# Six different byte offsets for the split weights of the narrow products

## The chip, the cores and the metric

The kernel runs on one core of a Trainium2 chip. The metric is the device time of one execution in microseconds (us). Before the change three runs gave 1155.51, 1155.75 and 1159.62 us, median 1155.75 us. About 0.5% (5.8 us) is what a measurement of this kernel can tell from no change.

## The reference

A decoder trunk of two layers over 512 tokens of width 1024, in float32. The first layer mixes with a gated delta rule, the second with sliding-window attention, both also attend to 256 memory tokens. Each layer ends in a gated feed-forward block, and this block is the part that matters here:

```
def swiglu(h, w_gate_up, w_down):
    gu = h @ w_gate_up
    return (jax.nn.silu(gu[..., :D_FF]) * gu[..., D_FF:]) @ w_down

x = x + swiglu(rms_norm(x, ln_ffn[layer]), w_gate_up[layer], w_down[layer])
```

D_FF is 2816, so the block has 22 column tiles of 128 for the gate and 22 for the up projection, and `w_down` goes back to 1024.

## The kernel before, in words

**Precision by three products.** TensorE multiplies in the type fp32r, which holds fewer bits than float32. So every float32 operand is split into a high part (ScalarE copies it to fp32r, line 148) and a low part (VectorE subtracts the high part from the original, line 161). `mm3` (line 206) then issues three matmuls for each 128x128 block of weights: high weight with high activation, high weight with low activation, low weight with high activation. Each matmul has its own load of 128 weight columns into the array (LDWEIGHTS), and it streams its moving operand, the activations, past them. In the trace both carry line 154, the load as PEld and the stream as PE.

**Wide and narrow matmuls.** Most projections stream 512 tokens per matmul (`project`, line 214, and the down projections). Most of the gate and up projections of the feed-forward block are done in another way: `quarters` (line 1005) multiplies two column tiles at once with seven smaller products in place of eight. Each of these seven products (`product`, line 1020) takes 512 columns of split weights (four blocks of 128) and streams 256 tokens, so it issues 4 x 3 = 12 narrow matmuls of 256 columns. Each half of each layer's block calls `quarters` ten times, 40 calls in all, hence 40 x 7 x 12 = 3360 narrow matmuls. The moving operands are halves of the normalised activations (`h`, `l`) and of sums of them, made by `token_sums` (line 979) and held in tiles that are called `T`.

**The ring.** The split weights of one product take 512 columns of a high tile and 512 of a low tile. `ffn` (line 870) takes three such pairs of tiles of 1024 + 64 columns from the pool (`parts`, line 190) and cuts each in two, which makes six places; `ring` (line 893) hands them out in turn, one for each product. With seven products per call and six places every place serves each of the seven kinds of product in turn. A place is free for ScalarE's next split when the 12 matmuls that read it are done.

**Where the bytes lie.** Tiles are padded to 64 bytes (line 104). In the built program every tile of moving operands of these products, and every weight tile, starts at 192 bytes modulo 256 in its row of on-chip memory (SBUF); halves of 256 tokens are 1024 bytes, blocks of 128 weight columns 512 bytes, so both keep that remainder. Before the change a ring part starts at column `SHIFT` = 52 of its tile, 208 bytes further, which puts it 48 bytes below its moving operand modulo 256. All other split weights are read from column 0: their distance to the moving operands is 0.

The work of one feed-forward block runs in this order: four gate tiles as wide products, then the narrow products without a break, then half of the down projection (wide), then the same again for the second half.

Of the kernel before, what the change touches and what calls it, by code (L numbers as in the profile page):

```python
# [19 lines left out]
T = 512  # L20
# [7 lines left out]
FT = DFF // P  # L28
EPS = 1e-6
LINE = 64  # L30
SHIFT, SPARE = 52, 64
NEG = -1e30
BASE = 32
NB = P // BASE
# [54 lines left out]
class Builder:  # L89
# [780 lines left out]
    def ffn(self, fp, xp, layer, h, apool, rope=False):  # L870
# [3 lines left out]
        acts, sums, open_pairs, places = [], [], [], []  # L874
# [18 lines left out]
        def ring():  # L893

            if not places:
                for _ in range(3):
                    two = self.parts()
                    places.extend(tuple(x[:, SHIFT + i * T:SHIFT + (i + 1) * T] for x in two) for i in range(2))
            places.append(places.pop(0))
            return places[-1]  # L900

        def begin(f, up, by, tag, bufs, then):

            o = [self.t(fp, [P, T], F32, tag, bufs) for _ in range(2)]
            steps = self.quarters(fp, [col(f + i, up) for i in range(2)], sums, by, o, ring)
            next(steps)
            end()
            next(steps)
            open_pairs.append((steps, then, o))
            return o  # L910
# [42 lines left out]
        if tail < KD:  # L953
# [9 lines left out]
            for t in parts:  # L963
                acc = self.acc[:, t]
                for m in range(tail, KD):
# [3 lines left out]
                    x = self.x[m][:, t]  # L969
# [301 lines left out]
```

## Time and profile before

| | |
|---|---|
| median of 3 runs | 1155.75 us |
| profiled execution, its own time | 1153.46 us |
| its span from the first to the last instruction | 1151.7 us |
| granted TensorE clock | 0.998 |
| TensorE streaming, share of the span | 98% |
| VectorE, ScalarE, GpSimd, share of the span | 73%, 55%, 7% |

One execution was recorded by the hardware profiler. PE is TensorE streaming matmuls, PEld the weight loads beside it, DVE is VectorE, ACT ScalarE, POOL GpSimd, SP the queue that issues most transfers. Matmuls overlap in the pipeline: a row's mean duration holds the latency from the first column in to the last one out, so what a stream of matmuls costs is read from the distance between their starts (called the pitch below), not from their durations. The chain of waits follows the program back from its last instruction; a row of it that holds many matmuls one after another, with the time from the first to the last, gives the mean pitch directly.

### The profile page before, as it was taken

The numbers are of one execution on the slowest core, as the hardware profiler recorded it, in microseconds if no ns is written. First come the engines' busy times: TensorE is split into PE (matmuls) and PEld (weight loads), VectorE is DVE, ScalarE is ACT, GpSimd is POOL, SyncE is SP. The second block draws the span as 40 slices with busy tenths as digits, with TensorE's granted clock in tenths as the row PEclk, the third lists the DMA queues.
The fourth block names the chain that finished last, engine by engine and source line by source line (L and its number), as shares of the span: only waits on it lengthen the run. The fifth ranks groups of instructions, "written<-read, shape, count | busy, mean of one in ns | idle before, by whom it ended". The sixth has DMA issues, their size and how long they took to land.

```text
span 1151.7 us, 19665 instructions
## 1 busy us (share of the span) xinstructions
PE 1129.2 (98%) x7476; PEld 990.3 (86%) x7476; DVE 842.4 (73%) x1587; ACT 632.1 (55%) x1271; POOL 86.1 (7%) x97
## 2 busy tenths in 40 slices
PE   7999999999999999999999999999999999999996
PEld 6888778887889998899998777778899988999986
DVE  5764877767789987389876767859799843898754
ACT  7579563366566652256654547675566622566533
POOL 0220000000111100011100000010011100111000
PEclk9999999999999999999999999999999999999999
DMA  8333342235557754567723421144478743577232
GB/s 310 118 121 110 120 101 95 85 106 162 167 138 186 191 126 127 160 147 187 181 69 103 134 79 38 40 110 129 115 186 193 180 112 103 147 190 184 70 95 93
DMA packets 73971, 152.83 MB, mean 133 GB/s; under 512 B 17756, under 2 KB 18420, under 8 KB 73876
## 3 DMA queue, kind: packets, MB, share of 16 engines
q1 hardware_dynamic: 62356, 130.59, 36.5%
q0 software_dynamic: 11520, 20.98, 11.6%
q8 instruction: 59, 0.97, 0.4%
q14 instruction: 36, 0.29, 0.1%
HBM read 144.58 MB, written 6.96 MB: 132 GB/s over the span
## 4 chain that ended last, share of the span: by engine, by line
PE 89%; DVE 6%; ACT 3%; DMA 1%; issue 1%; SPq 0%; DVEq 0%; ACTq 0%
PE pj L154 43%; PE g L154 38%; PE sc L154 5%; DVE wlo L161 2%; ACT sm L142 1%; PE pt L158 1%; PE qk L154 1%; ACT whi L148 1%; PE g L158 1%; DMA wraw<-in_wmk 1%; DVE stats L778 1%; DVE l L164 0%; DMA wraw<-in_win 0%; DVE x L164 0%; DVE btmp L161 0%
## 5 line engine op out<-in xcount | busy, mean ns | idle before, releaser
L148 ACT ACTIVATE whi<-wraw 128x512 fp32r<-128x512 f32 (+2 forms) x331 | 244.1, 746 | 253.6 <-PE pj L154 156.3
L161 DVE TENSOR_TENSOR wlo<-wraw,whi 128x512 fp32r<-128x512 f32 (+2 forms) x331 | 274.5, 839 | 104.7 <-ACT whi L148 98.4
L154 PE MATMUL pj<-h,whi 128*128 128x512 f32 (+1 forms) x676 | 266.4, 396 | 0.0
L154 PE MATMUL pj<-l,whi 128*128 128x512 f32 (+1 forms) x676 | 264.7, 392 | 0.4 <-DVE l L164 0.4
L154 PE MATMUL pj<-h,wlo 128*128 128x512 f32 (+1 forms) x676 | 264.0, 391 | 0.0
L154 PE MATMUL g<-T,whi 128*128 128x256 f32 x1280 | 228.1, 278 | 0.2
L154 PEld LDWEIGHTS g<-T,whi 128*128 128x128 f32 x1280 | 194.7, 188 | 1.8 <-DVE fu L164 1.8
L154 PE MATMUL g<-T,wlo 128*128 128x256 f32 x640 | 177.8, 278 | 0.0
L154 PEld LDWEIGHTS pj<-h,whi 128*128 128x128 f32 x676 | 126.8, 188 | 29.4 <-issue 3.6
L154 PEld LDWEIGHTS pj<-l,whi 128*128 128x128 f32 x676 | 127.1, 188 | 27.3 <-issue 1.8
L154 PEld LDWEIGHTS pj<-h,wlo 128*128 128x128 f32 x676 | 127.0, 188 | 25.7 <-issue 0.8
L154 PE MATMUL g<-l,whi 128*128 128x256 f32 (+1 forms) x508 | 144.4, 284 | 0.0
L154 PE MATMUL g<-h,whi 128*128 128x256 f32 (+1 forms) x508 | 144.3, 284 | 0.0
L154 PE MATMUL g<-h,wlo 128*128 128x256 f32 (+1 forms) x508 | 144.3, 284 | 0.0
L154 PEld LDWEIGHTS g<-T,wlo 128*128 128x128 f32 x640 | 120.1, 188 | 0.0
L154 PEld LDWEIGHTS g<-l,whi 128*128 128x128 f32 x508 | 95.3, 188 | 1.4 <-issue 0.2
L154 PEld LDWEIGHTS g<-h,whi 128*128 128x128 f32 x508 | 95.3, 188 | 1.2
L154 PEld LDWEIGHTS g<-h,wlo 128*128 128x128 f32 x508 | 95.3, 188 | 1.0
L1014 POOL DMA_DIRECT2D ws<-in_wgu x40 | 35.1, 877 | 707.9 <-DMA ws<-in_wgu 255.1
L148 ACT ACTIVATE whi<-ws 128x512 fp32r<-128x512 f32 x80 | 50.4, 630 | 49.0 <-PE g L154 40.2
L161 DVE TENSOR_TENSOR fu<-pj,rstd 128x512 f32<-128x512 f32 (+1 forms) x34 | 22.4, 660 | 54.2 <-PE pj L154 54.2
L161 DVE TENSOR_TENSOR wlo<-ws,whi 128x512 fp32r<-128x512 f32 x80 | 54.9, 686 | 6.4 <-ACT whi L148 6.3
(345 smaller groups left out, 1620.7 us busy)
## 6 DMA issues: line engine op xcount, KB each, us to landing
wraw<-in_wgu SPq DMA_DIRECT2D x48, 512.0 KB, 4.3
ws<-in_wgu SPq DMA_DIRECT2D x80, 256.0 KB, 3.5
ws<-in_wgu POOLq DMA_DIRECT2D x80, 256.0 KB, 4.7
wraw<-in_wdn SPq DMA_DIRECT2D x48, 384.0 KB, 3.1
wraw<-in_win SPq DMA_DIRECT2D x26, 512.0 KB, 3.6
wraw<-in_wgu SPq DMA_DIRECT2D x40, 256.0 KB, 4.5
wraw<-in_wout SPq DMA_DIRECT2D x16, 512.0 KB, 3.6
wraw<-in_wdn SPq DMA_DIRECT2D x16, 256.0 KB, 2.7
```

Source lines behind the costliest of these rows:

```text
L142: ins = self.nc.scalar.activation(out, in_, func, **kw).ins
L148: self.copied = self.nc.scalar.activation(out, in_, AF.Copy, **kw).ins
L154: return self.nc.tensor.matmul(out, lhsT, rhs, start=start, stop=stop, skip_group_check=more).ins
L158: return self.nc.tensor.transpose(out, in_, self.ident[:k, :k]).ins
L161: return eng.tensor_tensor(out=out, in0=a, in1=b, op=op).ins
L778: nc.vector.tensor_reduce(out=mx[:, i:i + 2], in_=ps[b], op=ALU.max, axis=AX.X)
L1014: nc.gpsimd.dma_start(s1, a22, accum_op=ALU.add)
```

## The change

The one shift of all six ring places becomes a shift of its own for each: 46, 55, 42, 53, 51 and 57 columns of 4 bytes, in the order in which the places are handed out. A part at column c starts 4c bytes above the start of its tile, so 256 - 4c bytes below its moving operand modulo 256: 72, 36, 88, 44, 52 and 28 bytes in place of 48 for all. High and low part of a place have the same distance.

```
-SHIFT, SPARE = 52, 64
+NARROW, SPARE = ((46, 55), (42, 53), (51, 57)), 64
...
             if not places:
-                for _ in range(3):
+                for shifts in NARROW:
                     two = self.parts()
-                    places.extend(tuple(x[:, SHIFT + i * T:SHIFT + (i + 1) * T] for x in two) for i in range(2))
+                    places.extend(tuple(x[:, o + i * T:o + (i + 1) * T] for x in two) for i, o in enumerate(shifts))
             places.append(places.pop(0))
             return places[-1]
```

The tiles have the same size and the same base address as before, and the instructions of each engine stand in the same order, row for row, with the same operands. Of the 3360 narrow matmuls 576 each then read weights at 72, 36, 88 and 44 bytes, and 528 each at 52 and 28. Before, all parts start at a multiple of 16 bytes; after, none does (remainders 8, 12, 8, 4, 12 and 4, as 192 + 4c modulo 16).

## The prediction

> **What bounds the kernel now.** I read the page's busy times first.
>
> ```profile
> span 1151.7 us, 19665 instructions
> PE 1129.2 (98%) x7476; PEld 990.3 (86%) x7476; DVE 842.4 (73%) x1587; ACT 632.1 (55%) x1271; POOL 86.1 (7%) x97
> ```
>
> TensorE is busy 98% of the span, so the question is whether the narrow matmuls wait for something or follow each other as fast as they can. The chain of waits answers it; its rows give start, length, work and count.
>
> ```profile
> 333.36 96.60 PE g L154 x828
> ...
> 432.74 64.17 PE pj L154 x283
> ...
> 823.50 96.60 PE g L154 x828
> ...
> 922.89 64.20 PE pj L154 x283
> ```
>
> The g rows are narrow matmuls, two of the four stretches with a ring. They lie in the chain unbroken: 828 matmuls in 96.60 us, 116.7 ns from start to start. The pj rows are wide ones (512 columns, distance 0): 64.20 us / 283 = 226.9 ns. What the helpers do in the same four stretches stands in the table of busy times by stretch (columns: sum of PE, PE, PEld, DVE, ACT, POOL, granted clock, share of the transfer engines, GB/s).
>
> ```profile
> 333.20:429.80 96.60, 96.60 (x830) 96.60 (x828) 86.31 (x156) 61.30 (x117) 12.97 (x15) 1.00 0.70 170
> 496.80:593.30 96.50, 96.50 (x829) 96.50 (x828) 84.89 (x152) 61.98 (x117) 13.00 (x15) 1.00 0.65 157
> 823.30:920.00 96.70, 96.70 (x830) 96.66 (x830) 85.81 (x154) 61.21 (x117) 16.46 (x19) 1.00 0.75 181
> 986.90:1083.50 96.60, 96.60 (x829) 96.57 (x828) 84.94 (x152) 61.99 (x117) 12.98 (x15) 1.00 0.64 157
> ```
>
> The clock is granted in full, VectorE is busy 85 to 86 us of 96.6, ScalarE 62. Who is ahead is seen in the groups by shape: the two rows of ScalarE that make high parts of 512 columns.
>
> ```profile
> L148 ACT ACTIVATE whi<-wraw 128x512 fp32r<-128x512 f32 x217 | 133.9, 629 | 84.8 <-PE g L154 38.1 <-PE pj L154 36.4 <-ACT fs L148 2.4
> L148 ACT ACTIVATE whi<-ws 128x512 fp32r<-128x512 f32 x80 | 50.4, 630 | 49.0 <-PE g L154 40.2 <-ACT fs L148 8.8
> ```
>
> Their idle time ends most often with a narrow matmul: the splits wait for a free place, TensorE does not wait for the splits. So the pitch of 3360 narrow matmuls is paid in full, 1 ns of it is 3.36 us of the kernel.
>
> **Does the offset matter at all?** This kernel has narrow matmuls at distance 0 too, those of the memory keys. The timeline shows them one by one; these are the first and the last of 40 in a row (start in us, then the modelled duration).
>
> ```profile
> 29.79 0.28 PE L154 MATMUL sc<-mh,wlo 128*128 128x256 f32 x1
> ...
> 34.47 0.28 PE L154 MATMUL sc<-mh,wlo 128*128 128x256 f32 x1
> ```
>
> 4.68 us over 39 steps is 120.0 ns. So at distance 0 the pitch is 120.0, at 48 it is 116.7. Now split that number. A wide matmul streams 256 more columns than a narrow one, and at distance 0 costs 226.9 - 120.0 = 106.9 ns more, which is the price of streaming 256 columns. What is left per matmul is an overhead of 120.0 - 106.9 = 13.1 ns at distance 0 and 116.7 - 106.9 = 9.8 ns at distance 48. That the distance makes this difference is an inference: the two groups also differ in stage and tiles, but have the same shapes, loads and types.
>
> The smallest overhead of a load that I find is in the transposes of the attention, whose moving operand is a constant: eight loads of 128 columns in a row.
>
> ```profile
> 757.33 0.90 PEld L158 LDWEIGHTS pt<-consts,sm 128*128 128x128 f32 x8 [0.60 <-ACT pf L148]
> L158 PEld LDWEIGHTS pt<-consts,sm 128*128 128x128 f32 x116 | 12.5, 140 | 6.5 <-ACT pf L148 2.7 <-issue 2.0 <-PE pj L154 0.8
> ```
>
> The second row gives 140 ns for one, so seven steps take 0.90 - 0.14 = 0.76 us, 109 ns each. That is the end below: a narrow matmul has to load 128 columns as well, so I take no pitch under 109.
>
> The end above comes from wide matmuls at distance 0 in another stage, first and last of ten.
>
> ```profile
> 80.27 0.40 PE L154 MATMUL pj<-l,whi 128*128 128x512 f32 x1
> ...
> 82.36 0.39 PE L154 MATMUL pj<-l,whi 128*128 128x512 f32 x1
> ```
>
> 2.09 us / 9 = 232.2 ns, 5.3 more than the 226.9 above at the same distance. So the pitch isn't fixed by the distance alone; the streams can also fall into a worse step with each other. The end above is 120.0 + 5.3 = 125.3 ns.
>
> **The change part by part.** Nothing is removed, added or moved in any engine's order; three things change address.
>
> *Splits that write the ring.* ScalarE and VectorE now write to starts that are not multiples of 16 bytes. VectorE has rows of that kind: the taps of the convolution write at 4, 8 and 12 bytes past an aligned start.
>
> ```profile
> L164 DVE SCALAR_TENSOR_TENSOR l<-x,gains,h 128x512 fp32r<-128x512 f32 x32 | 23.5, 748 | 1.5 <-ACT h L148 1.5
> L164 DVE SCALAR_TENSOR_TENSOR qv<-pj,gains,qv 128x511 f32<-128x511 f32 x12 | 9.0, 747 | 2.7 <-ACT qv L148 2.4
> L164 DVE SCALAR_TENSOR_TENSOR qv<-pj,gains,qv 128x509 f32<-128x509 f32 x12 | 8.9, 741 | 0.1
> ```
>
> 747 and 741 ns against 748 at an aligned start: no price. For ScalarE no row shows it. If a split took 10% more, 70 of them in a stretch would add 70 x 0.063 = 4.4 us to 62 busy ones of 96.6, which the idle rest covers. I cost this part at nothing. Without that cover it would be those 4.4 us in each of four stretches.
>
> *Weight loads of the ring.* This is the price that decides. The trace has a steady pitch at distances 0 and 48 only, for none of the six new ones. I assume that the effect repeats every 64 bytes, so that 64 is like 0 (an assumption; no row shows it), and draw straight lines between 120.0 at 0, 116.7 at 48 and 120.0 at 64, a difference of 3.3 ns. Distance 28 then gives +1.4 ns against 48, 36 gives +0.8, 44 +0.3, 52 +0.8; 72 counts as 8 and gives +2.8, 88 counts as 24 and gives +1.7. With the counts: 528 x (1.4 + 0.8) + 576 x (0.8 + 0.3 + 2.8 + 1.7) = 1162 + 3226 ns = 4.4 us. The mean pitch becomes 116.7 + 4.4 / 3.36 = 118.0 ns. Between the ends, 3360 x (109 - 116.7) = -25.9 us and 3360 x (125.3 - 116.7) = +28.9 us, I take this value because four of the six distances lie within 20 bytes of the measured 48 and the pitch there should resemble it.
>
> *Hand-over between products.* Every 12 matmuls the distance now jumps. Before it jumps from 48 to 0 where a stretch ends; these are the wide matmuls right behind the first stretch, the first and the fifth.
>
> ```profile
> 429.80 0.40 PE L154 MATMUL pj<-h,whi 128*128 128x512 f32 x1
> ...
> 430.71 0.39 PE L154 MATMUL pj<-l,whi 128*128 128x512 f32 x1
> ```
>
> Four steps take 0.91 us, by the rounding of the two starts at most 0.92; four steps of 226.9 ns are 0.908. A jump costs nothing to some 10 ns, 280 of them 0 to 2.8 us. Jumps of 8 to 52 bytes should cost less than this one, and some may help; I leave it out of the sum and in the range.
>
> The sum: 1153.46 + 4.4 = 1157.9 us for the profiled execution. The median of the three runs lies 2.3 us above that execution; 1155.75 + 4.4 gives 1160 us. That is 0.4%, inside 0.5% (5.8 us, what a measurement of this kernel can tell from no change).
>
> **A rule weighed.** The rows have 120.0 against 116.7 ns where shapes and types agree and the placement differs. The Trainium skill, page "TensorE: Matmul & The Clock Gate", section "Step-by-step: what each phase is for", says that TensorE has two independent read ports on SBUF, so that loading the next weights takes no bandwidth from the running matmul. By that the placement would change nothing and the time would stay at 1155.75 us. The two rows speak against it, as far as they differ in nothing else.
>
> Another one speaks against this change. The page "SBUF — State Buffer", section "Specifications (TRN2)", gives lines of 16 bytes and a penalty for each crossing to a new line. 512 bytes of weights that start off a line touch 33 lines, not 32; my estimate from this page and the overhead of 9.8 ns over 32 lines is 0.3 ns a matmul, 1 us in all. No run so far shows it.
>
> **The rivals.**
>
> *Slower: 48 is a good place and its neighbours are not.* If the 3.3 ns at 48 depend on whole 16-byte steps between the two streams, all six places, none of which is a multiple of 16 away, fall back to the 120.0 ns of distance 0: 3360 x 3.3 = 11.1 us, 1167 us. For it: 120.0 ns is exact over 39 steps, and the 232 ns row shows that worse steps exist. Against it: 48 to 44 and 52 is a small move. It decides against my forecast once the mean pitch passes 116.7 + 5.8 / 3.36 = 118.4 ns, which is only 0.4 above the forecast.
>
> *Faster: shifted by a part of 16 bytes the two streams stop meeting.* Parts that start 4 or 12 bytes off a multiple of 16 (36, 44, 52 and 28, 2208 matmuls) would come down to the 109 ns of the loads that meet nothing: 2208 x 7.7 = 17.0 us, 1139 us; half of it gives 1147 us. VectorE, at 86 us a stretch, would still fit in the 92 us left. For it: an overhead of 9.8 ns is there to be gained. Against it: no row shows a load at such an offset, and the two placements seen moved the pitch by 3 ns, not 8.
>
> *Nothing: the placement doesn't matter,* and the 3.3 ns come from the stage. Then 1155.75 us. For it: the two groups differ in stage. Against it: the narrow row holds 120.0 without spread, with the same shapes.
>
> **How the numbers follow.** Forecast (mean pitch 116.0 to 118.4) 0.39; nothing 0.06; slower rival and what lies above 118.4 ns 0.33; faster rival 0.22. So faster by over 0.5%: 0.22; within: 0.39 + 0.06 = 0.45; slower: 0.33. The range reaches from the half-way case of the faster rival, 1147 us, to the slower one with a microsecond on top, 1168 us; about 0.1 is left out at each end. The forecast alone would have 1153.4 to 1161.5: 3360 x (116.0 - 116.7) = -2.4 us and 3360 x (118.4 - 116.7) = 5.7 us from the median.
>
> **What would show it.** In the profile after, each of the four stretches of 828 narrow matmuls in the chain gives the mean pitch: 97.7 us is my forecast, 99.4 the slower rival, 92.4 or less the faster one, 96.6 no effect. Within a stretch the starts of 12 matmuls of a product show the pitch of each place: I expect the places at 72 and 88 slowest, 44 nearest to 116.7. A pitch off the line at 72 and 88 alone would fell the assumption of 64 bytes; 120 at 44 and 52 would prove the slower rival. ScalarE's rows for high parts should stay near 630 ns, VectorE's low parts near 690; PE waits in the stretches should stay absent. If the time moves while the pitch stays at 116.7, I have named the wrong resource.

## The result, and the profile after

The changed kernel took 1164.26, 1165.07 and 1166.47 us, median 1165.07 us, against 1155.75 us before: a ratio of 1.0082 with a 95% interval of 1.0062 to 1.0102. It is slower by 9.3 us, inside the predicted range of 1147 to 1168 us, but beyond the 5.8 us that the forecast of 1160 us still called no change. The profiled execution took 1166.47 us.

The page's busy times, as before:

```profile
span 1164.7 us, 19665 instructions
PE 1140.2 (98%) x7476; PEld 1001.0 (86%) x7476; DVE 845.7 (73%) x1587; ACT 632.3 (54%) x1271; POOL 86.0 (7%) x97
```

The span grew by 13.0 us, TensorE's busy time by 11.0, the helpers' by 3.3 and 0.2. The chain of waits shows where: the four stretches of narrow matmuls (start, length, work, count), with one wide stretch between them for comparison.

```profile
333.45 99.30 PE g L154 x828
435.51 64.16 PE pj L154 x283
499.67 99.30 PE g L154 x828
...
831.33 99.30 PE g L154 x828
...
997.54 99.30 PE g L154 x828
```

A stretch takes 99.30 us in place of 96.60; the wide one, whose addresses the change leaves alone, 64.16 as before. 99.30 / 828 = 119.9 ns is the new mean pitch, and 4 x 2.70 = 10.8 us is what the stretches add. The table of busy times by stretch has TensorE without a gap still, at a full clock (two of the four rows):

```profile
333.40:432.80 99.40, 99.40 (x830) 99.38 (x829) 87.49 (x156) 61.55 (x118) 12.94 (x15) 1.00 0.68 166
831.30:930.70 99.40, 99.40 (x830) 99.36 (x829) 86.90 (x154) 61.39 (x118) 16.42 (x19) 1.00 0.74 179
```

The splits into the shifted parts cost what they did, 630 and 633 ns on ScalarE, and still wait for places:

```profile
L148 ACT ACTIVATE whi<-wraw 128x512 fp32r<-128x512 f32 x217 | 135.5, 630 | 92.2 <-PE g L154 45.8 <-PE pj L154 35.4 <-ACT fs L148 2.5
L148 ACT ACTIVATE whi<-ws 128x512 fp32r<-128x512 f32 x80 | 50.6, 633 | 54.1 <-PE g L154 44.5 <-ACT fs L148 9.6
```

So TensorE itself runs slower, without waiting for anyone. Inside a product the pitch of each place is seen in the timeline; these are the first and the twelfth matmul of a product from the place at 52 bytes.

```profile
347.60 0.29 PE L154 MATMUL g<-h,whi 128*128 128x256 f32 x1
...
348.96 0.29 PE L154 MATMUL g<-h,wlo 128*128 128x256 f32 x1
```

1.36 us over 11 steps is 123 ns. Averaged over all products of a place, with the step to the next product, the starts give 119.7 ns at 28 bytes, 121.4 at 36, 117.5 at 44, 123.0 at 52, 118.1 at 72 and 119.9 at 88.

Outside the stretches the profiled execution lost 2.2 us more (13.0 - 10.8). The three executions of the changed kernel differ by as much among themselves, and the fastest of them, 1164.26 us, lies 10.8 us above the profiled one before. In the profile ScalarE waited longer for the output weights, in the row of that wait (us in total, times, longest) first before and then after:

```profile
ACT whi L148 <- DMA wraw<-in_wout: 8.2, 4, 2.9
```

```profile
ACT whi L148 <- DMA wraw<-in_wout: 10.6, 4, 4.4
```

That total lay between 4.2 and 10.4 us in the profiles of the experiments below, in no relation to their pitch. Why it differs, and whether it is what the 2.2 us are made of, stays open.

### The profile page after: what moved, and what is told of

Same layout as the page of the kernel before. It is cut to its first block, busy times and chain, and to the rows that moved or that the text cites. A ratio compares the mean times of both kernels' runs of the same rounds, so it can differ in the third digit from the quotient of the medians.

```text
span 1164.7 us, 19665 instructions
## 1 busy us (share of the span) xinstructions
PE 1140.2 (98%) x7476; PEld 1001.0 (86%) x7476; DVE 845.7 (73%) x1587; ACT 632.3 (54%) x1271; POOL 86.0 (7%) x97
## 4 chain that ended last, share of the span: by engine, by line
PE 87%; DVE 6%; ACT 3%; DMA 2%; issue 1%; SPq 0%; DVEq 0%; ACTq 0%
PE pj L154 41%; PE g L154 38%; PE sc L154 6%; DVE wlo L161 2%; ACT sm L142 1%; PE pt L158 1%; DMA wraw<-in_wout 1%; PE qk L154 1%; ACT whi L148 1%; PE g L158 1%; DVE l L164 1%; DMA wraw<-in_wmk 1%; DVE stats L778 1%; DVE T L161 0%; DVE x L161 0%
## 5 line engine op out<-in xcount | busy, mean ns | idle before, releaser
L161 DVE TENSOR_TENSOR wlo<-wraw,whi 128x512 fp32r<-128x512 f32 (+2 forms) x331 | 275.9, 842 | 106.9 <-ACT whi L148 100.2
L154 PE MATMUL g<-T,whi 128*128 128x256 f32 x1280 | 234.2, 283 | 0.0
L154 PEld LDWEIGHTS g<-T,whi 128*128 128x128 f32 x1280 | 197.1, 188 | 1.4 <-DVE fu L164 1.4
L154 PE MATMUL g<-T,wlo 128*128 128x256 f32 x640 | 180.5, 282 | 0.0
L154 PE MATMUL g<-l,whi 128*128 128x256 f32 (+1 forms) x508 | 147.3, 290 | 0.0
```

What stands on the lines that cost most here:

```text
L154: return self.nc.tensor.matmul(out, lhsT, rhs, start=start, stop=stop, skip_group_check=more).ins
L161: return eng.tensor_tensor(out=out, in0=a, in1=b, op=op).ins
```

## The experiments

**Distance 0 throughout.** It tests whether the difference between 120.0 and 116.7 ns, seen before in two different stages, comes from the distance.

```
-NARROW, SPARE = ((46, 55), (42, 53), (51, 57)), 64
+NARROW, SPARE = ((0, 0),) * 3, 64
```

> All six ring parts at distance 0, nothing else changed. Theory (the pitch of a narrow matmul is set by the distance between its weights and its moving operand modulo 256, place by place): the pitch seen at distance 0 in the memory keys, 120.0 ns, holds here too, so a stretch of 828 takes 99.4 us and the kernel is 3360 x 3.3 ns = 11 us slower than before. Rival (the 3.3 ns between the memory keys and the ring came from the stage, and the change is slower because its parts start off 16-byte lines or because the distance jumps at every product): no jumps and aligned starts here, so 116.7 ns, 96.6 us a stretch and no change.

Measured: 1164.4 us median, ratio to before 1.0066 (1.0046 to 1.0086). The first two stretches in the chain:

```profile
334.02 99.35 PE g L154 x828
500.33 99.35 PE g L154 x828
```

99.35 / 828 = 120.0 ns. Same stage, tiles, order and aligned starts; the distance alone costs 3.3 ns. The rival, that the stage made the difference, is out. The four stretches hold 4 x 2.75 = 11.0 us more than before, as expected; the medians differ by 7.4 us only. Among executions with a granted clock of 0.998 it is more, 1164.1 to 1164.5 us against 1154.4 and 1155.1; the rest is not explained.

**Distance 52 throughout.**

```
-NARROW, SPARE = ((46, 55), (42, 53), (51, 57)), 64
+NARROW, SPARE = ((51, 51),) * 3, 64
```

> All six parts at distance 52, the slowest place of the changed kernel (122.8 ns inside its products). Theory: 122.8 ns everywhere, 101.7 us a stretch of 828, 3360 x 6.1 ns = 21 us slower than before, slower than the change itself. Rival (jumps between distances cost the time): without jumps back to 116.7 ns, 96.6 us a stretch. Rival (any start off a 16-byte line costs the same): the mean of the changed kernel, 119.9 ns, 99.3 us a stretch, 11 us slower.

Measured: 1177.88 us, ratio 1.0186 (1.0162 to 1.021).

```profile
334.84 102.11 PE g L154 x828
503.80 102.11 PE g L154 x828
```

102.11 / 828 = 123.3 ns, 0.5 above the theory's value. Four bytes from 48 to 52 cost 6.6 ns a matmul, and no jump takes part in that.

**The other places one by one.** Two kernels give each stretch a distance of its own, the same for all six places of it.

```
-NARROW, SPARE = ((46, 55), (42, 53), (51, 57)), 64
+SPARE = 64
+SCAN = (((55, 55), (55, 55), (55, 55)), ((53, 53), (53, 53), (53, 53)), ((46, 46), (46, 46), (46, 46)), ((42, 42), (42, 42), (42, 42)))
...
-                for shifts in NARROW:
+                for shifts in SCAN[2 * layer + (f0 > 0)]:
```

> One distance for all six parts within a stretch, another in each stretch: 36, 44, 72, 88, four of the six distances of the change, now without jumps between products. Theory A (each distance has its pitch, whatever stands beside it): as in the changed kernel, 121.4, 117.5, 118.1 and 119.9 ns, that is 100.5, 97.3, 97.8 and 99.3 us a stretch. Theory B (the distance and the step in which load and stream enter a product decide together; the run with the T tiles moved spoke for it): each stretch settles into one repeating pattern, which may lie some ns off those values, above all at 36 and 88, which already differed between two kernels (121.4 and 120.0; 119.9 and 118.2); 44 and 72, which agreed within 0.4 ns, stay. Rival (the jumps between distances make the change slow): near 116.7 ns, 96.6 us, in all four.

Measured (one execution of 1163.15 us), stretches at 36, 44, 72 and 88; this kernel has one line more near its top, so the line numbers are one higher:

```profile
333.65 99.97 PE g L155 x828
500.61 97.15 PE g L155 x828
829.63 97.52 PE g L155 x828
994.11 99.36 PE g L155 x828
```

That is 120.7, 117.3, 117.8 and 120.0 ns. In the change the same places had 121.4, 117.5, 118.1 and 119.9. So without jumps they stay within 0.7 ns; the jumps are not what costs most of the time. Theory A describes these four.

The second kernel has 28, 176, 168 and 244 in the same way.

> The same with 28, 176, 168 and 244. Theory A: 120.0, 118.9, 115.2 and 116.4 ns as on the map (99.4, 98.4, 95.4 and 96.4 us a stretch). Theory B: 28 stays at 120.0, which every step but the entry showed; 168 settles at the 113.3 ns that it reached in its later steps, 93.8 us; 176 and 244 may come out anywhere between 113 and 120.

Measured (1156.93 us):

```profile
333.36 99.35 PE g L155 x828
499.68 98.25 PE g L155 x828
829.73 93.86 PE g L155 x828
990.56 93.83 PE g L155 x805
```

120.0, 118.7, 113.4 and 116.6 ns. 168 takes 113.4 where the map had averaged 115.2 with a slower start in each product; the other three agree with the map.

With the uniform stretches every place of the change has a price: 528 x ((120.0 - 116.7) + (123.3 - 116.7)) + 576 x ((120.7 - 116.7) + (117.3 - 116.7) + (117.8 - 116.7) + (120.0 - 116.7)) = 5.2 + 5.2 = 10.4 us. The stretches of the change added 10.8. If the 0.4 us left are the jumps at 280 products, a jump costs 1.4 ns; they are not measured apart from what a place's neighbours do to its pitch. (A stretch of 828 holds 69 of its 70 products; the last one runs among the wide matmuls behind it.)

**The two slow places put back.**

```
-NARROW, SPARE = ((46, 55), (42, 53), (51, 57)), 64
+NARROW, SPARE = ((46, 52), (42, 53), (52, 57)), 64
```

> The change with its two slowest places (36 and 52, measured at 121.4 and 123.0 ns) put back to 48, the other four kept. Theory A: 576 x 4.7 + 528 x 6.3 ns = 6.0 us less than the change, about 1159 us, 3.3 us slower than before. Theory B: less than the change as well, but the four kept places may shift by a few ns, since they now follow other neighbours. Rival (jumps): still as slow as the change, 1165 us, since the distance still jumps at every product.

Measured: 1159.36 us, ratio 1.0031 (1.0016 to 1.0045) to before. The first stretch in the chain:

```profile
334.98 97.69 PE g L154 x828
```

The other three take the same, 118.0 ns. Of the change's 10.8 us in the stretches 6.4 are gone (4 x (99.30 - 97.69)), where 6.0 were expected of the two places. The jumps are still there.

**The map.** Three kernels of the same kind as the uniform ones, but with six distances in each stretch, cover all 64 steps of 4 bytes.

> A map: each of the four stretches has six distances of its own, 24 in all (columns 0, 3, 6 ... 63, and 52 and 53, that is 0 to 256 bytes in steps of 12). Theory: each distance has a pitch of its own that shows in the starts of the 12 matmuls of a product; 48 comes out at 116.7, 52 at 122.8, 44 at 117.3, 72 at 118.2, 36 at 120.8 as in the kernels already seen, whatever their neighbours are. If the effect repeats every 64 bytes, distances that differ by 64 agree. Rival (jumps or line starts): no pattern in the distance, or one by its remainder of 16 alone.

> The map's second third: columns 1, 4, 7 ... 61, and 0, 46 and 51 once more. Theory: 72 and 52 repeat 118.2 and 122.8 ns, the others fill the gaps; pitches range from about 115 to 126 ns with no relation to whether a start is a multiple of 16. Rival (line starts): only the remainder modulo 16 decides, the same pitch for all parts with the same remainder.

> The map's last third: columns 2, 5, 8 ... 62, and 0, 52 and 36 once more (distances 8, 20, 32 ... 248, and 0, 48, 112). Theory: 0 gives 120.0, 48 116.6 and 112 119.4 ns once more. 180 gave 113.3 and 168 115.2 with 113.3 in its later steps, so 176 should lie near 113 too if the good places form a band, and be anything between 113 and 123 if each distance stands alone.

One execution each: 1165.32, 1160.36 and 1161.01 us. The pitch of a place is read from the starts of its products; these are the first and the twelfth matmul of one at 180.

```profile
1010.84 0.28 PE L155 MATMUL g<-h,whi 128*128 128x256 f32 x1
...
1012.09 0.28 PE L155 MATMUL g<-h,wlo 128*128 128x256 f32 x1
```

1.25 us over 11 steps, 113.6 ns by these two roundings and 113.4 over all its products, the lowest of the map. From the same starts some neighbours: 44 to 52 gave 117.5, 116.6 and 122.3 to 123.0; 164 to 184 gave 117.8, 115.2, 120.3, 118.9, 113.4 and 118.5. At 116, that is 52 + 64, it was 116.5, and at 112, 48 + 64, 119.5 and 120.1. So neither nearness nor a period of 64 bytes holds, and the remainder modulo 16 doesn't sort them: 180 (start 12 bytes off a line) is the fastest, 52 (also 12 off) the slowest of those above. That the distances are taken modulo 256 rests on two things: in the uniform runs at 0, 48 and 180 the six places, whose starts differ by multiples of 256 bytes, agree within 0.1 ns once a stretch is under way, and 52 and 180, which are 128 apart, do not agree. A few distances differed between kernels: 36 had 120.0 here and 121.4 in the change, 88 had 118.0 (116 and 120 in turn) and 119.9, 0 had 118.6 and 119.4 in two of the map's kernels and 120.0 elsewhere.

**The moving operands shifted.**

```
-NARROW, SPARE = ((46, 55), (42, 53), (51, 57)), 64
+NARROW, SPARE = ((51, 51),) * 3, 64
...
-            pool("edge", side="right").tile([P, 8], F32, name="edge")
+            pool("edge", side="right").tile([P, 24], F32, name="edge")
```

> All weight parts at column 51 as in the run with distance 52 throughout, but the unused tile at the right edge is 64 bytes longer, which moves the T tiles (moving operands of four of the seven products) down by 64 bytes and leaves the h and l tiles (the other three products) where they are. Weights have the same addresses as in that run. Theory (the distance of the two operands decides): the products from T stand at 244 and take 116.4 ns as on the map, the products from h and l stay at 52 and take 123 ns. Rival (the address of the weights itself, its start off a line, decides): 123 ns for all. The tiles ac8 to ac11 move as well, so some wide matmuls change their distance from 0 to 192.

Measured (1156.98 us), the first stretch in the chain:

```profile
331.87 96.43 PE g L154 x828
```

That is 116.5 ns. The theory had 4/7 x 116.4 + 3/7 x 123 = 119.2 ns, its rival 123; both are wrong. The weights have the same addresses as in the run at 52 throughout, so the weights' own address does not decide, and neither do the splits' writes, which go to those addresses. But the distance alone does not decide either: the products from T take 116 to 118 ns, near what was expected of 244, and those from `h` and `l`, whose distance is unchanged, are the ones that came out otherwise. These are the first and the twelfth matmul of three products from `h` and `l`, all at distance 52:

```profile
335.97 0.28 PE L154 MATMUL g<-h,whi 128*128 128x256 f32 x1
337.22 0.28 PE L154 MATMUL g<-h,wlo 128*128 128x256 f32 x1
337.34 0.28 PE L154 MATMUL g<-h,whi 128*128 128x256 f32 x1
338.58 0.28 PE L154 MATMUL g<-h,wlo 128*128 128x256 f32 x1
...
340.11 0.28 PE L154 MATMUL g<-h,whi 128*128 128x256 f32 x1
341.43 0.28 PE L154 MATMUL g<-h,wlo 128*128 128x256 f32 x1
```

Their 11 steps take 1.25, 1.24 and 1.32 us, so 114, 113 and 120 ns, each the same in every later call of `quarters`, where the uniform run at 52 had 123. What stands ahead of a product matters too.

**One odd place among six.** This separates the history from the distance, with no other tile moved.

```
-NARROW, SPARE = ((46, 55), (42, 53), (51, 57)), 64
+SPARE = 64
+SCAN = (((3, 51), (51, 51), (51, 51)), ((19, 51), (51, 51), (51, 51)), ((19, 51), (19, 19), (19, 19)), ((0, 19), (0, 0), (0, 0)))
...
-                for shifts in NARROW:
+                for shifts in SCAN[2 * layer + (f0 > 0)]:
```

> One of the six places at another distance than the other five: 244 among 52 in the first stretch, 180 among 52 in the second, 52 among 180 in the third, 180 among 0 in the fourth. Theory A: the five keep their own pitch, 123.1 ns at 52, 113.3 at 180, 120.0 at 0, also right behind the odd one. Theory B: the five products behind the odd place take on another pattern than in the uniform runs, at 52 then 113 to 120 ns in place of 123.1, and keep it over many matmuls.

Measured (1156.14 us), the four stretches in the chain:

```profile
334.93 101.17 PE g L155 x828
502.96 88.43 PE g L155 x780
827.02 93.86 PE g L155 x828
987.86 98.47 PE g L155 x828
```

The first two hold the same five places at 52. With one place at 244 a stretch takes 101.17 / 828 = 122.2 ns, and the starts give 123.5 ns for the five. With one place at 180 it is 88.43 / 780 = 113.4 ns, and all five places at 52 run at 113.3, over 60 matmuls up to the next odd place. So 52 has at least two steady patterns, 113.3 and 123, and what ran before chooses. In the fourth stretch 0 kept its 120.0 ns behind 180, and in the third 180 its 113.4 behind 52: these two did not show a second pattern. Theory B holds for 52, theory A for the others tried.

**Wide matmuls at all distances.** The ring stays at 48, the other split weights change their column with each pair of tiles.

```
-            hi, lo = (x[:, :n] for x in self.parts())
+            self.turn = (getattr(self, "turn", -1) + 1) % 64
+            hi, lo = (x[:, self.turn:self.turn + n] for x in self.parts())
```

> The ring as before (48), but the split weights of the wide projections start at another column for each pair of tiles, 0 to 63 in turn, so that the wide matmuls (227 ns at distance 0) are seen at all 64 distances. Theory (weight load and moving stream meet in the memory while both run): the wide matmuls depend on the distance in the same way, about 220 to 233 ns, best near 168 to 180, since a load lies beside the first half of each stream just as in the narrow ones. Rival (a wide matmul has time to spare and hides it): 227 ns at all distances.

Measured (1165.02 us). First and last of 24 wide matmuls at 180, then at 136:

```profile
112.78 0.39 PE L154 MATMUL pj<-h,whi 128*128 128x512 f32 x1
...
118.14 0.39 PE L154 MATMUL pj<-h,wlo 128*128 128x512 f32 x1
...
796.53 0.39 PE L154 MATMUL pj<-h,whi 128*128 128x512 f32 x1
...
801.75 0.40 PE L154 MATMUL pj<-h,wlo 128*128 128x512 f32 x1
```

23 steps take 5.36 and 5.22 us, 233 and 227 ns. The stage is not what makes the 233: in the kernel before, the first of these two rows of 24, at distance 0, starts and ends so:

```profile
113.19 0.39 PE L154 MATMUL pj<-h,whi 128*128 128x512 f32 x1
...
118.41 0.39 PE L154 MATMUL pj<-h,wlo 128*128 128x512 f32 x1
```

That is 5.22 us, 227 ns. Over all 64 distances the means run from 226.6 to about 237; distance 0 has 226.7 once a row has settled, and none lies clearly below it. So the wide ones depend on the distance as expected, but in another order: 180 is the best place for the narrow and a poor one for the wide, where column 0 already has the lowest pitch seen.

**Distance 180 throughout.**

```
-NARROW, SPARE = ((46, 55), (42, 53), (51, 57)), 64
+NARROW, SPARE = ((19, 19),) * 3, 64
```

> All six parts at distance 180 (column 19), the fastest place of the map, a start off a 16-byte line. Theory: 113.3 ns everywhere, 93.8 us a stretch, 3360 x 3.3 ns = 11 us faster than before: about 1145 us. VectorE at 86 us a stretch still fits. Rival (starts off a 16-byte line cost time): slower than before. Rival (the 113.3 ns come from what stood next to that place in the map): near 118 ns, 4 us slower than before.

Measured: 1143.78 us against 1154.38 of the kernel before on the same chip, ratio 0.9903 (0.9886 to 0.9921). Two stretches in the chain, then one in the table of busy times by stretch:

```profile
333.33 93.86 PE g L154 x828
...
818.50 93.86 PE g L154 x828
```

```profile
333.30:427.20 93.90, 93.90 (x830) 93.90 (x829) 85.68 (x156) 60.84 (x118) 13.10 (x16) 1.00 0.72 175
```

113.4 ns in place of 116.7 gives 3360 x 3.3 = 11.1 us; the medians differ by 10.6. It is also faster than the change, and VectorE, busy 85.7 us of 93.9, is covered as expected. 113.4 is half of the 226.7 ns that a wide matmul takes for twice the columns, so at this distance a narrow one costs no more per column than a wide one.

## Why the prediction was right or wrong

**What bounds the stretches: right.** The pitch of the narrow matmuls is paid in full. Four stretches grew by 2.70 us each, and the kernel by 9.3 us in the median.

**The inference from 120.0 and 116.7 ns: right.** Distance 0 in the ring's own stage gave 120.0 ns.

**The split of the pitch, and the two ends: misread.** The price of streaming 256 columns was taken as 226.9 - 120.0 = 106.9 ns, and so 9.8 ns of a narrow matmul at 48 passed for overhead. The narrow one at distance 0 that was subtracted carries an overhead itself. Measured against the 113.4 ns of the run at 180, which is half of a wide one's 226.7, the overhead at 48 is 3.3 ns and at 0 it is 6.6; no place came below 113.3, and the lower end of 109 was never near. The upper end took ten wide matmuls at 80.27 us for a steady pitch of 232.2. They follow directly on four transposes; from the tenth on the same row goes on like this:

```profile
82.36 0.39 PE L154 MATMUL pj<-l,whi 128*128 128x512 f32 x1
...
84.62 0.39 PE L154 MATMUL pj<-h,wlo 128*128 128x512 f32 x1
```

10 steps take 2.26 us, 226 ns. So at distance 0 the row settled within ten matmuls, and the 5.3 ns on top were the way there. That a stream can run in a worse step at the same distance came true nevertheless, at 52 bytes, but this row did not show a lasting one.

**The splits: right.** 630 and 633 ns against 629 and 630; the starts off a 16-byte line cost nothing there.

**The price of the six places: wrong, and this is the step that failed.** The term was +4.4 us, from straight lines between 0, 48 and an assumed 64; it measured 10.4 us. Place by place the forecast was +1.4, +0.8, +0.3, +0.8, +2.8 and +1.7 ns for 28, 36, 44, 52, 72 and 88; uniform stretches gave +3.3, +4.0, +0.6, +6.6, +1.1 and +3.3. Two things behind the lines were false. Distances near 48 need not resemble it: 44 does, 52 is 6.6 ns slower, more than distance 0. And the effect doesn't repeat every 64 bytes. My pick, that 72 and 88 would be the slowest, failed: 52 and 36 were, and 72 was the second fastest; 44 was indeed nearest to 48. All that was measured lies between the ends of 109 and 125.3 ns, though both were misread. With the true prices the sum gives 1166 us; the forecast of 1160 us and no visible change did not come, and it is the slower rival's end of the range that took the result in.

**The hand-over between products: right to leave out.** 0 to 2.8 us were named, and 0.4 are left after the places' own prices.

**The slower rival: its size came true, its mechanism didn't.** It named 99.4 us a stretch, and 99.30 was measured. But its places should all have fallen back to 120.0 ns, because none is a whole 16-byte step away. 28 and 88 did, 44 and 72 stayed near 117.5, 36 and 52 went past 120. That the mean is 119.9 is luck: it is made of places between 117.3 and 123.3.

**The faster rival: it exists, but not at these places.** It asked for 4 or 12 bytes off a multiple of 16 and named 36, 44, 52 and 28. 180 starts 12 bytes off a line and runs at 113.4, but 52 starts 12 off too and runs at 123; the remainder doesn't choose. Its gain was too large as well: 3.3 ns a matmul was there, not 7.7.

**The rules weighed.** In one stage, with the same shapes and order, the runs have 113.4 ns at 180, 116.7 at 48, 120.0 at 0 and 123.3 at 52. The Trainium skill, page "TensorE: Matmul & The Clock Gate", section "Step-by-step: what each phase is for", has the loads take no bandwidth from the running matmul. By that alone the placement would change nothing; it does, and the measurement decides. The line rule of the Trainium skill, page "SBUF — State Buffer", section "Specifications (TRN2)", a penalty for each crossing to a new line, would by itself have made 180 slower than 48; 180 is the fastest, so a price of the 33rd line is not seen.

**What is argued only.** That weight load and moving stream meet in the memory while both run fits all of this: the relative address counts, moving the activations changes the pitch as moving the weights does, and a pattern can persist from product to product. No run shows the collision itself, or how the memory is divided. Which distances are good was found by trying, not derived.

## What to carry to other kernels

Where TensorE runs without a gap and its pitch lies above what the columns alone cost (here half of the 226.7 ns of a matmul with twice the columns), the byte distance between weights and moving operands is worth a scan, in steps of the element size and with the neighbours it will have, since one kernel can carry a different distance in each stage and the trace prices them all. Don't interpolate between measured distances: 4 bytes moved the pitch by 6.6 ns of 117, more than the whole difference between the two values I had. Narrow and wide matmuls need a scan each. Read a steady pitch only after the first ten or so matmuls of a row.

## What the runs showed of the hardware that I had not expected

- With all else equal, the pitch of 256-column fp32r matmuls with a load each ranged from 113.4 ns (distances 168 and 180) to 123.3 ns (52) by the distance modulo 256.
- A distance can have two steady patterns. At 52 bytes five places ran at 113.3 ns where a product at 180 stood ahead of them and at 123.5 where one at 244 did, over 60 matmuls and in each round.
- For matmuls of 512 columns the order of the distances is another one: 233 ns at 180, 227 at 0 and 136.
- A row of these at distance 0 took 232 ns a step over nine steps right behind four transposes, and 226 to 227 from then on.
